# Thirty-two columns of an adaptation vector moved from VectorE and GpSimd to TensorE, in a hybrid decoder layer

## The chip, the cores and the metric

The program runs on one core of a Trainium2 chip. A core has five engines that run side by side, each with its own in-order queue: PE (TensorE, matrix products), DVE (VectorE), ACT (ScalarE), POOL (GpSimd) and SP (SyncE, which here only issues DMAs). They meet through semaphores. The metric is device time in microseconds (us) of one launch, the median of several runs.

## What is computed

One layer of a decoder trunk, for one sequence of 1024 tokens and a model width of 1024, all in float32. Cut to what matters here:

```
c_act = silu(c)                                  # 1024 values
mod = c_act @ w_ada + b_ada                      # w_ada is 1024 x 6144
shift1, scale1, gate1, shift2, scale2, gate2 = split(mod, 6)
h = rms_norm(x, norm1_w) * (1 + scale1) + shift1
proj = h @ w_in                                  # delta-rule heads and window heads
... gated delta rule (chunked, triangular solve) and sliding-window attention ...
x = x + gate1 * (concat(o_g, o_s) @ w_out)
h2 = rms_norm(x, norm2_w) * (1 + scale2) + shift2
x = x + gate2 * ((silu(h2 @ w_gate) * (h2 @ w_up)) @ w_down)
```

The adaptation vector `mod` has 6144 values. The kernel keeps it as 48 columns of 128 values in a tile `modc` (128 x 48): columns 0 to 15 are shift1 and scale1, which the very first stage needs; columns 16 to 47 are gate1, shift2, scale2 and gate2, which are needed much later (gate1 first, after the output projection).

## The kernel before, in words

Activations lie transposed, with the 1024 features as 8 tiles of 128 partitions and the tokens along the free axis, in two halves of 512. Each dense product is done as three fp32r products (the weight and the activation are each split into a high and a low part), so one *dense step* is three matmuls of 128 x 512, and a unit is eight such steps into one PSUM bank; a *skv* unit has steps of three matmuls 128 x 272. The generator `dense` hands out these steps; `fill(n)` puts n of them into PE's queue. PE's order is written out by hand (`manual_schedule`), the other engines' order is set by a scheduler when the program is built.

The order of the work, and the stretches that the prediction names:

- **Start.** Columns 0 to 15 of `modc` on DVE (`start_col`, L438), norm 1 and the first units.
- **Stretch A.** The rest of `h` (`modulate1`, L330 to L337: POOL, ACT and DVE), and a loop of 14 rounds, each with `fill(6)` and two columns of `modc` by `ada_some`: one by POOL (L256, a product of 128 x 1024) with a summing copy on ACT (L257), one by DVE alone (L253, a product with sum, 128 x 1024). A small DVE add of the bias (L259) follows each. Every column first needs its 512 KB of `w_ada`, loaded by SP into rings of two buffers with the tags b, c, d and e. Meanwhile DVE does the causal convolutions of the dense units (`conv`, L363 to L371: three long sums that read PSUM, three short ones for the seam L371, and the `tails` copy L368), which free the PSUM banks. A ends when PE reaches `psg` (L666), the cumulative sum of the decays, whose input `tsc` DVE makes (L641 to L661).
- **Stretch B.** The four head pairs (`pair_gen`), with dense steps between their visits.
- **Stretch C.** The triangular solve on DVE (`solve`, L817 and L820, about 60 short operations in a chain), with the window queries' norms between them; in it also the last four of the 32 columns (three on POOL, one on DVE).
- **After C.** `merge` and `scan_chunk`, the attention, the output projection and the feed-forward part.

The bank helper `sm` turns over four PSUM banks; `t2` is a ring of three 128 x 512 scratch tiles; `t4` gives the 512 KB tiles.

Of the kernel before, what the change touches and what calls it, by code (L numbers as in the profile page):

```python
# [54 lines left out]
def tile_hybrid_layer(  # L55
# [4 lines left out]
    rowvec: bass.AP,  # L60
    ada: bass.AP,
    wmain: bass.AP,
    wskv: bass.AP,
# [56 lines left out]
    def bc(ap, shape):  # L120
        return ap.broadcast_to(list(shape))
# [123 lines left out]
    def load_ada(u, tag=None):  # L245
        adat[u] = t4(f"ada{u}", tag=tag)
        done["ada"] = sp.dma_start(out=adat[u], in_=ada[u])

    def mod_col(u, eng=dve, bias=True):

        w = adat.pop(u)
        if eng is dve:
            dve.tensor_tensor_reduce(out=w, in0=w, in1=cb, scale=1.0, scalar=0.0, op0=ALU.mult, op1=ALU.add,  # L253
                                     accum_out=modc[:, u:u + 1])
        else:
            eng.tensor_tensor(out=w, in0=w, in1=cb, op=ALU.mult)  # L256
            act.activation(out=w, in_=w, func=AF.Copy, accum_out=modc[:, u:u + 1])  # L257
        if bias:
            dve.tensor_tensor(out=modc[:, u:u + 1], in0=modc[:, u:u + 1], in1=b_ada[:, u:u + 1], op=ALU.add)  # L259

    ada_next = [16]

    def ada_some(n, tag, eng=dve):
        for u in range(ada_next[0], ada_next[0] + n):
            if "kd" in done:
                with tc.issue_after(done["kd"].ins):
                    load_ada(u, tag)
            else:
                load_ada(u, tag)
            mod_col(u, eng)  # L270
        ada_next[0] += n

# [617 lines left out]
    def val(p):  # L890
        run(value_gen(p))

    for i in range(ADA_ITER):
        fill(VISITS_A[0])
        with tc.issue_after(h_done[0].ins), tc.issue_after(h_done[1].ins):
            ada_some(1, ADA_TAGS[2 * i], pool if i not in ADA_DVE else dve)
            ada_some(1, ADA_TAGS[2 * i + 1])
    next(token)
# [47 lines left out]
    for n, visit in zip(VISITS_B, (v0, v1, v2, v3, q0, q0, q1, q1, q2)):  # L946
        fill(n)
        next(visit)
        if visit is v3:
            for i in range(32 - 2 * ADA_ITER):  # L950
                ada_some(1, "b", pool if i % 4 else dve)
    dve.scalar_tensor_tensor(out=a2, in0=modc[:, 32:40], scalar=1.0, in1=n2w, op0=ALU.add, op1=ALU.mult)
# [701 lines left out]
```

## Time and profile before

| | |
|---|---|
| median of 3 runs | 1319.54 us (1319.52, 1319.54, 1326.32) |
| the profiled execution | 1316.65 us, its span 1314.9 us |
| PE, DVE, ACT, POOL busy share of the span | 91%, 68%, 41%, 48% |
| mean granted TensorE clock | 0.96 |

The span runs from the first to the last instruction; 1.75 us lie around it. Shares over the whole span hide the stages: from about 345 us on PE is nearly always busy, before that DVE is. PE records of a fp32 matmul come in twos (two passes), those of a fp32r matmul alone. A granted clock of 1.00 is 2.4 GHz, 0.50 is 1.2 GHz, and what lies between is a mean over a stretch.

### The profile page before, as it was taken

The numbers are of one execution on the slowest core, as the hardware profiler recorded it, in microseconds if no ns is written. First come the engines' busy times: TensorE is split into PE (matmuls) and PEld (weight loads), VectorE is DVE, ScalarE is ACT, GpSimd is POOL, SyncE is SP. The second block draws the span as 40 slices with busy tenths as digits, with TensorE's granted clock in tenths as the row PEclk, the third lists the DMA queues.
The fourth block names the chain that finished last, engine by engine and source line by source line (L and its number), as shares of the span: only waits on it lengthen the run. The fifth ranks groups of instructions, "written<-read, shape, count | busy, mean of one in ns | idle before, by whom it ended". The sixth has DMA issues, their size and how long they took to land.

```text
span 1314.9 us, 18979 instructions
## 1 busy us (share of the span) xinstructions
PE 1192.7 (91%) x6710; PEld 974.5 (74%) x6710; DVE 892.6 (68%) x1690; ACT 538.8 (41%) x1028; POOL 629.4 (48%) x453
## 2 busy tenths in 40 slices
PE   6867697896999799997998999999999999999998
PEld 5757576684788678785786788777777888888887
DVE  7999989979724677576646416877876875546430
ACT  4373555422434777434356432222232334544430
POOL 4667344534335444344354455545455545455440
PEclk8899799898999899998899999999999999999999
DMA  8727468485639865366845625556665567775651
GB/s 326 233 85 273 144 132 227 133 229 183 199 126 205 132 113 165 106 218 216 288 157 187 207 95 203 208 200 228 212 212 201 176 217 281 250 252 195 201 168 40
DMA packets 167214, 250.62 MB, mean 191 GB/s; under 512 B 40656, under 2 KB 106448, under 8 KB 165584
## 3 DMA queue, kind: packets, MB, share of 16 engines
q1 hardware_dynamic: 157520, 241.03, 56.6%
q0 software_dynamic: 9600, 8.39, 3.9%
q8 instruction: 53, 0.87, 0.3%
q14 instruction: 41, 0.34, 0.1%
HBM read 182.89 MB, written 66.45 MB: 190 GB/s over the span
## 4 chain that ended last, share of the span: by engine, by line
PE 43%; DVE 16%; DMA 8%; issue 4%; POOL 3%; ACT 3%; SPq 0%; DVEq 0%; ACTq 0%; POOLq 0%
PE ps_P L1359 5%; PE ps_P L1358 5%; PE ps_P L1360 5%; DMA wb<-in_wgate_dram 4%; PE ps_S L1358 2%; PE ps_S L1359 2%; PE ps_S L1360 2%; PE ps_c L1358 2%; PE ps_c L1359 2%; POOL wS L193 2%; PE ps_c L1360 2%; DVE wa L1427 1%; PE ps_gz L212 1%; DMA SD<-sd 1%; DVE soltmp L817 1%
## 5 line engine op out<-in xcount | busy, mean ns | idle before, releaser
L193 POOL TENSOR_TENSOR wP<-rP,wP 128x512 fp32r<-128x512 f32 (+1 forms) x84 | 108.3, 1301 | 105.3 <-ACT wP L192 100.2
L1359 PE MATMUL ps_P<-t,wP 128*128 128x512 f32 x308 | 120.4, 391 | 0.0
L1358 PE MATMUL ps_P<-t,wP 128*128 128x512 f32 x308 | 120.4, 391 | 0.0
L1360 PE MATMUL ps_P<-t,wP 128*128 128x512 f32 x308 | 120.2, 390 | 0.0
L193 POOL TENSOR_TENSOR wS<-wa,wS 128x512 fp32r<-128x512 f32 x44 | 62.8, 1437 | 111.8 <-ACT wS L192 78.9
L1360 PE MATMUL ps_S<-T,wS 128*128 128x512 f32 x264 | 102.8, 390 | 0.3 <-POOL wS L193 0.3
L1359 PE MATMUL ps_S<-T,wS 128*128 128x512 f32 x264 | 102.9, 390 | 0.0
L1358 PE MATMUL ps_S<-T,wS 128*128 128x512 f32 x264 | 102.9, 390 | 0.0
L192 ACT ACTIVATE wP<-rP 128x512 fp32r<-128x512 f32 (+1 forms) x84 | 48.4, 590 | 77.6 <-PE ps_P L1360 49.2
L1358 PE MATMUL ps_c<-B,w 128*128 128x512 f32 x176 | 70.5, 401 | 6.1 <-ACT X L1398 6.1
L1360 PE MATMUL ps_c<-B,w 128*128 128x512 f32 x176 | 69.7, 396 | 0.0
L1359 PE MATMUL ps_c<-B,w 128*128 128x512 f32 x176 | 69.7, 396 | 0.0
L1465 ACT ACTIVATE sg<-sg 128x512 f32<-128x512 f32 x33 | 20.9, 632 | 116.0 <-DVE sg L1461 116.0
L1358 PEld LDWEIGHTS ps_P<-t,wP 128*128 128x128 f32 x308 | 57.9, 188 | 12.6
L1360 PEld LDWEIGHTS ps_P<-t,wP 128*128 128x128 f32 x308 | 57.9, 188 | 12.5
L1359 PEld LDWEIGHTS ps_P<-t,wP 128*128 128x128 f32 x308 | 57.8, 188 | 12.4
L192 ACT ACTIVATE wS<-wa 128x512 fp32r<-128x512 f32 x44 | 26.7, 624 | 94.6 <-DVE wa L1426 71.8
L1424 DVE TENSOR_TENSOR ws<-wb 128x512 f32<-128x512 f32 x22 | 23.1, 1051 | 62.1 <-DMA wb<-in_wgate_dram 54.5
L1360 PEld LDWEIGHTS ps_S<-T,wS 128*128 128x128 f32 x264 | 49.6, 188 | 11.1 <-POOL wS L193 0.7
L212 PE MATMUL ps_o<-mix,w_o 128*128 128x512 f32 x128 | 53.7, 420 | 4.2 <-ACT w_o L192 4.2
L1358 PEld LDWEIGHTS ps_S<-T,wS 128*128 128x128 f32 x264 | 49.6, 188 | 10.5
L1359 PEld LDWEIGHTS ps_S<-T,wS 128*128 128x128 f32 x264 | 49.6, 188 | 10.5
(507 smaller groups left out, 3559.4 us busy)
## 6 DMA issues: line engine op xcount, KB each, us to landing
ada<-in_ada_dram SPq DMA_DIRECT2D x48, 512.0 KB, 4.7
AD<-ops SPq DMA_DIRECT2D x11, 1536.0 KB, 5.0
rP<-SD SPq DMA_DIRECT2D x16, 704.0 KB, 5.7
sd<-in_wdown_dram SPq DMA_DIRECT2D x20, 512.0 KB, 5.3
SD<-sd SPq DMA_DIRECT2D x20, 512.0 KB, 3.9
rP<-in_wdown_dram SPq DMA_DIRECT2D x12, 704.0 KB, 5.3
XD<-X SPq DMA_DIRECT2D x22, 256.0 KB, 3.3
xu<-XD SPq DMA_DIRECT2D x22, 256.0 KB, 3.4
```

The costliest lines, as they stand in the source:

```text
L192: act.activation(out=r(hi), in_=src, func=AF.Copy)
L193: last = eng.tensor_tensor(out=r(lo), in0=src, in1=hi, op=ALU.subtract)
L212: pe.matmul(out, lhsT=r(lhs[0]), rhs=r(rhs[0]), start=first, stop=False)
L817: dve.tensor_tensor(out=tv[g], in0=bc(L[:, i, i + 1:32].unsqueeze(1), (P, i, 31 - i)), in1=bc(L[:, 0:i, i:i + 1], (P, i, 31 - i)), op=ALU. ...
L1358: pe.matmul(ps, lhsT=r(wh), rhs=r(xh), start=first and i == 0, stop=False, **kw)
L1359: pe.matmul(ps, lhsT=r(wh), rhs=r(xl), start=False, stop=False, **kw)
L1360: pe.matmul(ps, lhsT=r(wl), rhs=r(xh), start=False, stop=i == n - 1, **kw)
L1424: dve.tensor_tensor(out=s1, in0=a21, in1=a22, op=ALU.add)
L1427: dve.tensor_tensor(out=a12, in0=a12, in1=a11, op=ALU.subtract)
L1465: act.activation(out=out, in_=out, func=AF.Silu)
```

## The change

All 32 columns go to PE. Four columns make a group: `ada_gen` issues, for each of its 4 column tiles, 8 fp32 matmuls with 32 stationary columns (the same column of `c` 32 times over) and 128 moving ones; matmul k goes to the column group k mod 4 of the array (`tile_position`), so PSUM holds four partial sums, in partitions 0, 32, 64 and 96. ACT copies the bank to a scratch tile (`ada_row`), and four matmuls with one moving column (`sel`, 1 in those four partitions) add the four sums up and turn the row into columns; one DVE add puts in the bias for all four. A group is done in four steps (two tiles of matmuls, two more, the copy, the sums), and the loop takes three steps after each `fill(6)` from the fourth round on. All 32 loads of `w_ada` are set out ahead of the loop; the weights lie in DRAM in the layout of the other weights, 4 KB in a piece as before.

```diff
+    sel = cp.tile([P, 1], F32, name="sel")
+    pool.memset(sel, 0.0)
+    for g in range(4):
+        pool.memset(sel[32 * g:32 * g + 1], 1.0)
     ada_next = [16]
-    def ada_some(n, tag, eng=dve):
-        for u in range(ada_next[0], ada_next[0] + n):
-            ...
-                load_ada(u, tag)
-            mod_col(u, eng)
+    def ada_load(tag):
+        ...
+        adat[u] = t4(f"ada{u}", (P, KT, P), tag=tag)
+        with tc.issue_after((done["kd"] if "kd" in done else done["x"]).ins):
+            sp.dma_start(out=adat[u], in_=ada2[u - 16])
+    def ada_gen(u0, q=None):
+        ps = sm(f"ps_ada{u0}", q)
+        for m in range(2):
+            for n in (2 * m, 2 * m + 1):
+                w = adat.pop(u0 + n)
+                for k in range(KT):
+                    g = k % 4
+                    pe.matmul(ps[32 * g:32 * g + 32, n * P:(n + 1) * P], lhsT=bc(c_col[:, k:k + 1], (P, 32)), rhs=w[:, k],
+                              start=k < 4, stop=k >= 4, tile_position=(0, 32 * g))
+            yield
+        row = t2(f"ada_row{u0}")
+        act.activation(out=row, in_=ps, func=AF.Copy)
+        yield
+        for n in range(4):
+            pe.matmul(ps[:, n:n + 1], lhsT=row[:, n * P:(n + 1) * P], rhs=sel, start=True, stop=True)
+        dve.tensor_tensor(out=modc[:, u0:u0 + 4], in0=ps[:, 0:4], in1=b_ada[:, u0:u0 + 4], op=ALU.add)
+        yield
...
+    adas = chain(*(ada_gen(16 + 4 * i) for i in range(8)))
+    for tag in ADA_TAGS:
+        ada_load(tag)
     for i in range(ADA_ITER):
         fill(VISITS_A[0])
-        with tc.issue_after(h_done[0].ins), tc.issue_after(h_done[1].ins):
-            ada_some(1, ADA_TAGS[2 * i], pool if i not in ADA_DVE else dve)
-            ada_some(1, ADA_TAGS[2 * i + 1])
+        for _ in range(3 if i >= 3 else 0):
+            next(adas, None)
+    run(adas)
...
-        if visit is v3:
-            for i in range(32 - 2 * ADA_ITER):
-                ada_some(1, "b", pool if i % 4 else dve)
```

PE's queue in stretch A, inside the second half of the unit `gk2` (the key projection of pair 2), before:

```order
L212 MATMUL ps_gk2_1_855<-h2_132,w_gk2h_635 128x512
L213 MATMUL ps_gk2_1_855<-h2_132,w_gk2h_635 128x512
L214 MATMUL ps_gk2_1_855<-h2_132,w_gk2l_636 128x512
L212 MATMUL ps_gk2_1_855<-h3_133,w_gk2h_635 128x512
L213 MATMUL ps_gk2_1_855<-h3_133,w_gk2h_635 128x512
```

and after:

```order
L213 MATMUL ps_gk2_1_898<-h2_138,w_gk2h_641 128x512
L214 MATMUL ps_gk2_1_898<-h2_138,w_gk2h_641 128x512
L215 MATMUL ps_gk2_1_898<-h2_138,w_gk2l_642 128x512
L286 MATMUL ps_ada16_917<-ada16_760,sml_99 32x128 x8
L286 MATMUL ps_ada16_917<-ada17_762,sml_99 32x128 x8
L286 MATMUL ps_ada16_917<-ada18_764,sml_99 32x128 x8
L286 MATMUL ps_ada16_917<-ada19_766,sml_99 32x128 x8
L213 MATMUL ps_gk2_1_898<-h3_139,w_gk2h_641 128x512
L214 MATMUL ps_gk2_1_898<-h3_139,w_gk2h_641 128x512
```

Between two dense steps stand the 32 small matmuls of the first group (columns 16 to 19; `sml` holds `c`), and nothing else has moved on PE here: the dense steps keep their order.

At the end of the last skv unit two of the eight groups have their third and fourth step without dense steps between them; after the change PE's queue reads there (the group of columns 36 to 39; `gk0_1` is the next dense unit):

```order
L215 MATMUL ps_skv7_1242<-wk_hi_154,h3_139 128x272
L286 MATMUL ps_ada36_1256<-ada38_804,sml_99 32x128 x8
L286 MATMUL ps_ada36_1256<-ada39_806,sml_99 32x128 x8
L293 MATMUL ps_ada36_1256<-sel_130,ada_row36_1310 128x1 x4
L213 MATMUL ps_gk0_1_1322<-h0_136,w_gk0_1_1317 128x512
```

The sums (L293) read `ada_row36`, which ACT makes from the two rows just above.

POOL's queue in stretch A before (`xt` are the last products of `modulate1`, `w_` the splits of weights):

```order
L334 TENSOR_TENSOR xt6_1_567<-xt6_1_567,row_n1_1_684 128x512
L256 TENSOR_TENSOR ada16_776<-ada16_776,cb_119 128x1024
L256 TENSOR_TENSOR ada20_846<-ada20_846,cb_119 128x1024
L256 TENSOR_TENSOR ada22_874<-ada22_874,cb_119 128x1024
L256 TENSOR_TENSOR ada18_811<-ada18_811,cb_119 128x1024
L256 TENSOR_TENSOR ada26_947<-ada26_947,cb_119 128x1024
L256 TENSOR_TENSOR ada34_1067<-ada34_1067,cb_119 128x1024
L256 TENSOR_TENSOR ada28_977<-ada28_977,cb_119 128x1024
L193 TENSOR_TENSOR w_gq0_1_1153<-w_gq0_1r_1154,w_gq0_1_1153 128x1024
```

and after:

```order
L358 TENSOR_TENSOR xt6_1_573<-xt6_1_573,row_n1_1_690 128x512
L194 TENSOR_TENSOR w_gq0_1_1390<-w_gq0_1r_1391,w_gq0_1_1390 128x1024
L194 TENSOR_TENSOR w_gk1_1_1467<-w_gk1_1r_1468,w_gk1_1_1467 128x1024
L194 TENSOR_TENSOR w_gq1_1_1546<-w_gq1_1r_1547,w_gq1_1_1546 128x1024
L194 TENSOR_TENSOR w_gk3_0_1658<-w_gk3_0r_1659,w_gk3_0_1658 128x1024
```

Only the four splits of weights are left to POOL in the rest of A.

## Rows read from the trace of the kernel before

**Rows 1.** Stretches A and C: length; PE, PEld, DVE, ACT, POOL busy; clock, DMA.

```profile
77.20:157.70 80.50, 53.07 (x260) 44.97 (x259) 79.91 (x126) 40.31 (x80) 50.62 (x22) 0.87 0.52 183
...
285.40:345.00 59.60, 43.84 (x206) 35.95 (x204) 59.04 (x171) 15.23 (x25) 22.83 (x14) 0.89 0.58 182
```

**Rows 2.** Waits of PE, 77 to 346 us: us in total, times, longest.

```profile
PE psr_s L725 <- ACT wide_s L721: 15.0, 2, 13.4
PE psg L666 <- DVE tsc L661: 12.1, 1, 12.1
...
PE ps_gk L212 <- ACT kq L387: 8.6, 1, 8.6
```

**Rows 3.** Timeline, 85 to 97 us: start, duration, engine, line, operation [idle before, releaser].

```profile
85.00 5.17 POOL L256 TENSOR_TENSOR ada<-ada,cb 128x1024 f32<-128x1024 f32 x2
...
85.12 5.59 DVE L332 SCALAR_TENSOR_TENSOR h<-xt,modc,h 128x512 fp32r<-128x512 f32 x2
...
92.61 0.74 DVE L332 SCALAR_TENSOR_TENSOR h<-xt,modc,h 128x512 fp32r<-128x512 f32 x1
...
96.93 0.77 PE L212 MATMUL ps_gk<-h,w_gk2h 128*128 128x512 f32 x1 [8.59 <-ACT kq L387]
```

**Rows 4.** PE in A by group of instructions, and its timeline: dense matmuls back to back.

```profile
L213 PE MATMUL ps_skv<-wk_lo,h 128*128 128x272 f32 x33 | 10.1, 306 | 0.0
...
103.93 0.39 PE L212 MATMUL ps_gq<-h,w_gq 128*128 128x512 f32 x1
104.16 0.39 PE L213 MATMUL ps_gq<-h,w_gq 128*128 128x512 f32 x1
...
112.02 0.29 PE L212 MATMUL ps_skv<-wk_hi,h 128*128 128x272 f32 x1
112.14 0.29 PE L213 MATMUL ps_skv<-wk_lo,h 128*128 128x272 f32 x1
```

**Rows 5.** Timeline of PE at fp32 matmuls with two column groups, and with none.

```profile
71.22 0.95 PE L321 MATMUL ssps<-ones,sq 128*128 128x1 f32 x8
...
197.40 2.37 PE L781 MATMUL psA<-kq,kn 64*64 64x128 f32 x59
...
212.02 1.09 PE L781 MATMUL psA<-kq,kn 64*64 64x128 f32 x16 [0.16 <-ACT sq_q L710]
213.04 0.50 PE L212 MATMUL ps_gv<-h,w_gv 128*128 128x512 f32 x1
...
362.48 1.16 PE L1039 MATMUL pk<-S,kvq 128*128 128x128 f32 x8
```

**Rows 6.** Timeline of ACT in A.

```profile
109.90 0.67 ACT L363 ACTIVATE qt<-ps_gq,sml 128x512 f32<-128x512 f32 x1
110.47 1.05 ACT L192 ACTIVATE w_gq<-w_gq_1r 128x1024 fp32r<-128x1024 f32 x1
...
132.88 1.28 ACT L643 ACT_TABLE_LOAD   x1
```

**Rows 7.** DMA issues by line: count, KB each, median us to landing.

```profile
ada<-in_ada_dram SPq DMA_DIRECT2D x48, 512.0 KB, 4.7
```

**Rows 8.** Timeline of PE just behind `psg`.

```profile
160.46 0.63 PE L213 MATMUL ps_gk<-h,w_gk 128*128 128x512 f32 x1
```

**Rows 9.** Timeline of POOL and DVE in C.

```profile
306.19 1.21 DVE L253 CUSTOM_DVE_ANT_0 ada<-ada,cb 128x1024 f32<-128x1024 f32 x1
...
311.42 0.38 DVE L820 TENSOR_TENSOR lanes<-lanes,soltmp 128x234 f32<-128x234 f32 x1
...
311.58 5.00 POOL L256 TENSOR_TENSOR ada<-ada,cb 128x1024 f32<-128x1024 f32 x2 [10.41 <-DVE soltmp L817]
...
312.33 2.00 DVE L820 TENSOR_TENSOR lanes<-lanes,soltmp 128x234 f32<-128x234 f32 x1
...
314.25 2.59 DVE L817 TENSOR_TENSOR soltmp<-lanes 128x238 f32<-128x238 f32 x1
...
320.46 2.34 DVE L184 TENSOR_TENSOR rsq_s<-rsq_s 128x16 f32<-128x16 f32 x1
```

More of the change, by code (lines that the diff above doesn't have):

```diff
@@ L61, in tile_hybrid_layer @@
     ada: bass.AP,
+    ada2: bass.AP,
     wmain: bass.AP,
@@ L259, in mod_col @@
             dve.tensor_tensor(out=modc[:, u:u + 1], in0=modc[:, u:u + 1], in1=b_ada[:, u:u + 1], op=ALU.add)
+    sel = cp.tile([P, 1], F32, name="sel")
+    pool.memset(sel, 0.0)
+    for g in range(4):
+        pool.memset(sel[32 * g:32 * g + 1], 1.0)
     ada_next = [16]
-    def ada_some(n, tag, eng=dve):
-        for u in range(ada_next[0], ada_next[0] + n):
-            if "kd" in done:
-                with tc.issue_after(done["kd"].ins):
-                    load_ada(u, tag)
-            else:
-                load_ada(u, tag)
-            mod_col(u, eng)
-        ada_next[0] += n
+    def ada_load(tag):
+        u = ada_next[0]
+        ada_next[0] += 1
+        adat[u] = t4(f"ada{u}", (P, KT, P), tag=tag)
[18 more added lines that the diff above has]
+        yield
     def rstd(ps, name):
@@ L1632 @@
         "rowvec": _np.concatenate([f["a_log"][0], f["dt_bias"][0], f["sinks"][0]]),
-        "ada": w_ada.T.reshape(48, P, D),
+        "ada": w_ada[:, 0:2 * D].T.reshape(16, P, D),
+        "ada2": tiles(w_ada[:, 2 * D:]),
         "wmain": tiles(_np.concatenate([w_in[:, 512:1024], w_in[:, 0:512], w_in[:, 1024:2048], w_in[:, 2064:2576]], axis=1)),
```

## The prediction

> **What bounds the kernel now.** I read the windows by stretch first, then PE's waits, then the timelines where a wait ends. In stretch A (77.2 to 157.7 us, up to `psg`) DVE is busy 79.9 of 80.5 us while PE is busy 53.1 and idle 27.4; in stretch C (285.4 to 345 us) DVE is busy 59.0 of 59.6 [rows 1]. So both are DVE's, and the reader is to see that POOL and ACT are not full in either. PE's long waits say the same: 12.1 us for `tsc` at the end of A, 8.6 us in A for a bank, 13.4 us in C for `wide_s`, whose input DVE makes [rows 2]. From 345 us on PE is busy nearly all the time, in an order that stays: what A and C gain or lose goes through to the end. Between them (stretch B) nothing is taken out.
>
> DVE's time in A is more than its own work. While POOL ran two of the `ada` products (5.17 us), two DVE operations with two SBUF inputs took 5.59 us together; one alone takes 0.74 [rows 3]. In C it is the same: beside POOL's products three short DVE operations took 2.00, 2.59 and 2.34 us, where one of the kind takes 0.38 [rows 9]. A POOL product thus costs DVE time as well as its own.
>
> **Stretch A after the change.** DVE loses its 14 products, most of its 28 bias adds and 14 POOL products beside it, so it stops being the limit, and A becomes a sum over PE's queue.
>
> Dense work: of the 260 PE records in A about 98 are of the 272-wide kind (33 on one of three lines), so 162 are 512 wide [rows 1, 4]. Back to back they follow each other at 0.2275 us (103.93 to 104.16, the mean over the units) and 0.126 us (112.02 to 112.14) [rows 4]. 162 x 0.2275 + 98 x 0.126 = 49.2 us, and 1.0 us for a stretch at the lower clock behind the wait that stays.
>
> The small matmuls: 256 fp32 matmuls, 512 records, in 16 steps of 32. The trace has none with four column groups; `psA` has the nearest: two column groups of 64. There a bank of 16 records, so eight rounds of two, took 1.02 us from its first start to the next dense matmul (212.02 to 213.04); `pk`, with no groups, took 1.16 us for eight records [rows 5]. With four groups running together a step of 32 is eight rounds of four, so again 1.02 us, and 0.1 us more for the restart of the dense matmuls behind it (0.50 against 0.39 in the row at 213.04 [rows 4, 5]): 1.12. Six steps follow another without dense work between and save 0.2 each: 16 x 1.12 - 1.2 = 16.7 us. Bounds: two groups at a time give 1.02 + 0.87 more a step (eight further rounds of 0.109, which is 1.02 less some 0.15 of start, over eight), 30.6 us; no overlap at all, at 1.16/8 = 0.145 a record, 74 us; below, rounds of four with no start and no restart, 512/4 x 0.109 = 14.0 us. The longest run of `psA`, 59 records in 2.37 us, 0.040 each [rows 5], would give 20.6. I take 16.7, from the single bank, the row nearest in shape to a step.
>
> The Trainium skill ("TensorE: Matmul & The Clock Gate", part 3 on packing) gives 2.38 times for three column tiles, not three; as an estimate from that page, four would give about 3.2, and the 16 steps 3.5 us more. No row here shows four tiles. The same page (steps of a matmul, decode) speaks of about 62 ns per matmul when the sequencer decodes in microcode; as an estimate from it the 512 records could not take less than 32 us, which would make this slower. The trace does not agree: 40 ns a record in `psA` [rows 5].
>
> The sums: four matmuls with one moving column are what `ssps` is, 0.95 us for eight records [rows 5]: 8 x 0.95 = 7.6 us.
>
> Waits of PE that stay or come. The bank wait at 96.93 ends when DVE has got through the operations stalled by POOL; without two products, and a third beside a `modulate` step, DVE is about 5.0 us earlier, and 8.6 - 5.0 = 3.6 us stay [rows 3]. New is PE's wait for ACT's copy; everything dense stands behind it in PE's queue. For six groups dense steps lie between, about 4.1 us (18 x 0.2275) or 2.3 us in skv (18 x 0.126). For the groups of columns 24 and 36 none do: the copy (about 0.65, as the 512-wide 0.67 [rows 6]) and hand-overs cost 0.9; and at column 36 a table load of 1.28 [rows 6] and the skv copies stand ahead of it on ACT, 2.5. At columns 20 and 44 a weight split of 1.05 and a 0.67 copy [rows 6] stand ahead on ACT while only two dense steps cover it: 1.7 and 1.3. Together 6.4 us. The bounds are 0 and, should the copy also queue behind a Silu that waits for DVE, about twice that.
>
> The loads are the same 512 KB each, landing 4.7 us after issue [rows 7]; they now wait for PE to release buffers six to eight tiles back, and four move up from C, ahead of two weight loads on SP. A group takes PE 2 x 1.12 + 0.95 and its dense steps, 6 to 8 us, so a load issued six tiles ahead is there; cost nothing, and if that cover goes, a landing less the cover, some 1 us a step.
>
> Sum: 49.2 + 1.0 + 16.7 + 7.6 + 3.6 + 6.4 = 84.5, against 80.5: A is 4.0 us longer. It also no longer ends in a wait of 12.1 us, behind which PE ran at the lower clock (0.63 a matmul instead of 0.39, about seven of them [rows 4, 8], 1.2 GHz against 2.4): 1.4 us back. `tsc` is off the path then: its inputs are there after the last skv unit, some 25 us of PE work ahead of `psg`.
>
> **Stretch C after the change.** It loses one DVE product (1.21), three short adds with it (0.3 together) and three POOL products. The stalls beside those fall from 2.00, 2.59 and 2.34 to about 0.4, 0.4 and 0.2 [rows 9]: 1.6 + 2.2 + 2.1. Together 7.4 us, all on the solve's chain; PE's 13.4 us wait [rows 2] shrinks with it, and the solve's result, which `merge` waits for, comes as much earlier. POOL's split of `w_sq` in the same place stays and goes on stalling DVE once.
>
> **Stretch B** is taken as unchanged. The scheduler has reordered DVE there (convolutions of `gk3` earlier), with the same operations; I allow 3 us either way.
>
> **Sum:** +4.0 - 1.4 - 7.4 = -4.8 us on the profiled execution, 1316.65 to 1311.9; on the median of the runs shown, 1319.54, that is 1314.7. I forecast 1315 us.
>
> **Rivals.**
> *Two groups at a time (slower).* The array takes only two of the four column groups together. For it: the rows show no more than two column groups. Against: nothing in them shows the second group costing the first anything. A step costs 1.89 us and PE 13.9 us more: -4.8 + 13.9 = +9, 1329 us. It decides from a step of about 1.4 us on, where A's loss eats C's gain. With no overlap at all, +52, 1372 us.
>
> *Loads late.* PE stands for `w_ada` in most of the 16 steps, about 1 us in 8 of them; DMA is at 0.52 of its time in A [rows 1], which speaks against. +3, 1323 us: no change that can be told.
>
> *PE's own waits do not come (faster).* ACT, which loses about 17 us in A and C, makes the copies in time, and the bank wait goes with DVE's relief: 6.4 + 3.6 us less, and A is shorter than before. For it: ACT is busy only half of A [rows 1]. Against: ACT's order has the splits ahead. -15, 1305 us; half of it, -10, 1310.
>
> *No gain from C.* PE reaches `merge` no earlier because other work in C holds it. PE's 13.4 us wait speaks against. Then +3, 1322 us.
>
> **How the numbers follow.** The measurement can tell about 0.5%, 6.6 us, from no change. Chances: forecast with its own spread (1311 to 1319) 0.40; two groups 0.19, no overlap 0.03; loads late 0.06; no gain from C 0.06; PE's waits gone 0.26. Faster by over 0.5% (under 1312.9): the last and a little of the forecast, 0.30. Slower (over 1326.1): 0.22 and a little, 0.24. Between: 0.46. The range 1304 to 1331 takes in the full rival of each sign.
>
> **What would show it.** In the profile after: the 32 records of a step in about 0.9 us and nearly 17 us for all 16 (right) or 1.7 us a step (two groups); PE idle in A about 10 us, with `ada_row` as releaser, and no wait for `tsc`; DVE no longer full in A; in C no DVE operation of 2 us at `soltmp` and `lanes` but one or two, the wait for `wide_s` near 6 us; the stretch from the first window query to `merge` earlier by A's change less 7. Wrong would be: A longer by over 10 us, a PE wait for `ada` loads, or a stretch B that changes by more than 3 us.

## The result, and the profile after

The changed kernel takes 1333.2 us (median of 8 runs, 1329.2 to 1340.3) against 1319.5 us of the kernel before in the same comparison (8 runs, 1317.3 to 1327.7): a ratio of 1.0092, 95% interval 1.0063 to 1.0121 (worked out from all the runs; it is not the ratio of the two medians). It is slower by 0.9%, where 1315 us and 1304 to 1331 were forecast. The profiled execution of after is one of 1329.16 us with a span of 1326.1 us, 12.5 and 11.2 us more than the one of before.

All lines of the kernel are 1 (at the top) to 24 further down than before, so L213 to L215 are the dense matmuls, L286 the small matmuls of `w_ada`, L290 the copy `ada_row`, L293 the sums. The page's line of busy time:

```profile
PE 1217.0 (92%) x7286; PEld 997.6 (75%) x7286; DVE 848.6 (64%) x1636; ACT 525.2 (40%) x1002; POOL 594.9 (45%) x441
```

DVE, ACT and POOL all have less to do, PE 576 records more (512 small, 64 of the sums). The stretches A, B and C by windows, after (columns as in [rows 1]), each from the first instruction of the stretch to that of the next. B and C meet here at the last unit of `psA`, and C goes to `merge`, so C begins earlier and ends later than in [rows 1]:

```profile
76.40:165.90 89.50, 80.23 (x836) 68.21 (x835) 40.67 (x83) 31.58 (x61) 14.87 (x8) 0.92 0.52 185
165.90:285.90 120.00, 94.95 (x601) 77.44 (x599) 101.24 (x178) 55.57 (x83) 52.78 (x24) 0.91 0.60 154
285.90:360.80 74.90, 67.55 (x371) 55.49 (x370) 64.73 (x194) 20.27 (x30) 34.01 (x21) 0.95 0.68 194
```

and B and C of before, cut at the same instructions:

```profile
157.70:271.90 114.20, 97.99 (x598) 80.31 (x598) 101.14 (x184) 56.65 (x84) 52.70 (x24) 0.91 0.62 161
271.90:353.90 82.00, 66.21 (x372) 54.77 (x372) 72.10 (x200) 23.60 (x36) 33.90 (x24) 0.92 0.65 195
```

In A DVE falls from 79.9 us of work to 40.7, and yet A grows from 80.5 to 89.5 us; PE is now busy 80 of it. B grows by 5.8 us with the same work, C shrinks by 7.1. `merge` starts 6.9 us later (360.8 against 353.9), so 4 us more are lost behind it, where nothing was changed.

PE's waits in A after, and the timeline of PE at the first group and at the longest wait:

```profile
PE ps_ada L293 <- ACT ada_row L290: 5.7, 4, 2.6
PE ps_gk L213 <- DVE tails L392: 3.6, 1, 3.6
```

```profile
96.99 1.95 PE L286 MATMUL ps_ada<-ada,sml 128*32 128x128 f32 x64
98.87 0.50 PE L213 MATMUL ps_gk<-h,w_gk2h 128*128 128x512 f32 x1
...
139.66 1.55 PE L293 MATMUL ps_ada<-sel,ada_row 128*128 128x1 f32 x8 [2.61 <-ACT ada_row L290]
141.07 0.77 PE L213 MATMUL ps_gk<-h,w_gk 128*128 128x512 f32 x1
141.64 0.63 PE L214 MATMUL ps_gk<-h,w_gk 128*128 128x512 f32 x1
142.06 0.63 PE L215 MATMUL ps_gk<-h,w_gk 128*128 128x512 f32 x1
```

The 64 records of two steps take 1.88 us to the next dense matmul: the four column groups run side by side. The waits are those forecast, 3.6 and 5.7 us. But behind the wait of 2.61 us the sums take 1.55 us where 0.95 is usual, and the dense matmuls show 0.63 each and follow each other at 0.43 us (141.64 to 142.06), where [rows 4] has 0.39 and 0.23: the lower clock, as in [rows 8]. The granted clock is 0.50 from 140.0 to 146.9 us; before that it is 0.50 from 92.3 to 95.7 us, behind the bank wait, and from 112.7 to 116.2 us, behind an `ada_row` wait of 1.46 us. Behind the other two `ada_row` waits, of 0.8 and 0.9 us, it stays at 1.00.

All kernels of this study in one table. A runs from the first `ps_gk` of the unit gk2_0 to `psg`, B to the last unit of `psA`, C to `psm`, the first matmul of `merge`; then comes scan and attention, to the last `psS`; 119 to 124 us later, in every kernel, the feed-forward part begins with the first `ps_c`. Microseconds of the profiled execution; time and ratio are from all runs beside the kernel before on the same chip. That kernel's own median was 1319.5 to 1322.7 us there, so kernels of different comparisons are compared by their ratios. Before and after have two profiles.

| kernel | median | ratio (95%) | A | B | C | `merge` at | scan | feed-f. | PE records |
|---|---|---|---|---|---|---|---|---|---|
| before | 1319.5 | | 80.5, 80.3 | 114.2, 114.0 | 81.9, 82.4 | 353.9, 354.3 | 171.8, 175.1 | 667.0, 667.4 | 6710 |
| after | 1333.2 | 1.0092 (1.0063-1.0121) | 89.5, 89.7 | 119.9, 121.5 | 75.0, 75.0 | 360.8, 365.2 | 177.5, 175.9 | 668.6, 674.2 | 7286 |
| b_order | 1331.6 | 1.0058 (1.0030-1.0086) | 86.3 | 115.8 | 75.0 | 354.8 | 177.1 | 675.2 | 7286 |
| a_dummy | 1321.4 | 0.9996 (0.9969-1.0022) | 85.4 | 116.2 | 75.0 | 356.6 | 175.3 | 671.4 | 7354 |
| a_cover | 1328.5 | 1.0058 (1.0025-1.0090) | 86.5 | 117.4 | 74.8 | 357.7 | 176.1 | 674.2 | 7286 |
| a_cover2 | 1326.7 | 1.0043 (1.0017-1.0069) | 78.8 | 115.4 | 75.0 | 346.7 | 177.8 | 677.2 | 7286 |
| c_only_p | 1326.6 | 1.0050 (1.0021-1.0080) | 82.2 | 119.1 | 79.0 | 357.7 | 176.6 | 674.3 | 6782 |
| hold | 1334.5 | 1.0094 (1.0061-1.0126) | 89.4 | 114.1 | 74.7 | 355.6 | 184.2 | 672.9 | 7286 |
| hold_dummy | 1320.2 | 0.9975 (0.9949-1.0001) | 83.4 | 111.4 | 75.0 | 347.1 | 177.5 | 667.7 | 7354 |
| hold_cover | 1319.4 | 0.9984 (0.9958-1.0009) | 78.1 | 112.0 | 75.0 | 342.6 | 179.8 | 673.2 | 7286 |
| hybrid | 1311.4 | 0.9912 (0.9882-0.9943) | 71.5 | 117.3 | 74.9 | 342.4 | 178.2 | 666.8 | 6998 |
| hold_hybrid | 1311.4 | 0.9916 (0.9880-0.9951) | 78.2 | 110.6 | 75.0 | 341.9 | 176.4 | 669.6 | 6998 |
| best | 1315.5 | 0.9962 (0.9931-0.9992) | 71.8 | 115.2 | 74.8 | 339.0 | 187.6 | 673.7 | 6998 |
| before_split | 1322.5 | 0.9995 (0.9968-1.0022) | 79.7 | 112.1 | 82.3 | 351.8 | 179.1 | 668.9 | 6710 |
| before_sel | 1321.7 | 1.0008 (0.9982-1.0034) | 80.3 | 114.3 | 81.8 | 353.6 | 175.5 | 665.3 | 6710 |
| hold_one | 1331.8 | 1.0080 (1.0045-1.0116) | 89.9 | 111.4 | 75.0 | 356.1 | 182.1 | 676.2 | 7286 |
| before_72 | 1328.5 | 1.0045 (1.0019-1.0071) | 80.4 | 113.6 | 82.5 | 356.1 | 174.9 | 672.2 | 6782 |
| hold_68 | 1327.4 | 1.0042 (1.0013-1.0072) | 90.0 | 115.6 | 75.0 | 359.4 | 174.9 | 672.4 | 7354 |

"Lost at the lower clock" below is worked out from windows of 2 us: PE's busy time in each with a granted clock under 0.97, times one minus that clock, summed over the stretch.

### The profile page after: what moved, and what is told of

Read it like the earlier page. It is cut to its first block, busy times and chain, and to the rows that moved or that the text cites. A ratio compares the mean times of both kernels' runs of the same rounds, so it can differ in the third digit from the quotient of the medians.

```text
span 1326.1 us, 20037 instructions
## 1 busy us (share of the span) xinstructions
PE 1217.0 (92%) x7286; PEld 997.6 (75%) x7286; DVE 848.6 (64%) x1636; ACT 525.2 (40%) x1002; POOL 594.9 (45%) x441
## 3 DMA queue, kind: packets, MB, share of 16 engines
q1 hardware_dynamic: 157520, 241.03, 55.7%
## 4 chain that ended last, share of the span: by engine, by line
PE 44%; DVE 15%; DMA 8%; issue 3%; POOL 3%; ACT 2%; SPq 0%; DVEq 0%; ACTq 0%; POOLq 0%
PE ps_P L1382 5%; PE ps_P L1384 5%; PE ps_P L1383 5%; DMA wb<-in_wgate_dram 3%; PE ps_S L1382 2%; PE ps_S L1383 2%; PE ps_S L1384 2%; PE ps_c L1382 2%; PE ps_c L1384 2%; PE ps_c L1383 2%; POOL wS L194 2%; DMA SD<-sd 1%; DVE soltmp L841 1%; PE ps_gz L213 1%; PE ptr L1070 1%
## 5 line engine op out<-in xcount | busy, mean ns | idle before, releaser
L194 POOL TENSOR_TENSOR wP<-rP,wP 128x512 fp32r<-128x512 f32 (+1 forms) x84 | 109.3, 1313 | 103.8 <-ACT wP L193 98.6
L1383 PE MATMUL ps_P<-t,wP 128*128 128x512 f32 x308 | 119.9, 389 | 0.0
L1382 PEld LDWEIGHTS ps_P<-t,wP 128*128 128x128 f32 x308 | 57.8, 188 | 12.1
L193 ACT ACTIVATE wS<-wa 128x512 fp32r<-128x512 f32 x44 | 26.6, 623 | 93.4 <-DVE wa L1450 86.3
L1448 DVE TENSOR_TENSOR ws<-wb 128x512 f32<-128x512 f32 x22 | 24.8, 1129 | 60.4 <-DMA wb<-in_wgate_dram 54.5
L1384 PEld LDWEIGHTS ps_S<-T,wS 128*128 128x128 f32 x264 | 49.6, 188 | 11.2 <-POOL wS L194 0.7
L213 PE MATMUL ps_o<-mix,w_o 128*128 128x512 f32 x128 | 52.6, 411 | 4.3 <-ACT w_o L193 4.3
```

The costliest lines, as they stand in the source:

```text
L193: act.activation(out=r(hi), in_=src, func=AF.Copy)
L194: last = eng.tensor_tensor(out=r(lo), in0=src, in1=hi, op=ALU.subtract)
L213: pe.matmul(out, lhsT=r(lhs[0]), rhs=r(rhs[0]), start=first, stop=False)
L1382: pe.matmul(ps, lhsT=r(wh), rhs=r(xh), start=first and i == 0, stop=False, **kw)
L1383: pe.matmul(ps, lhsT=r(wh), rhs=r(xl), start=False, stop=False, **kw)
L1384: pe.matmul(ps, lhsT=r(wl), rhs=r(xh), start=False, stop=i == n - 1, **kw)
```

## The experiments

### A second profile of each

No edit.

> The kernel before, once more, for a second profile of it: the parts up to merge should agree with the first within 2 us, and the part from the first psO on (881.2 us in the first, against 887 to 893 us in four of the changed kernels) tells whether the first was a lucky one. Theory (the late part only draws a different number of stretches at 1.2 GHz each time): 881 to 892 us. Rival (the late part is longer in every kernel with the change): 881 us within 1.5 us again.

> The changed kernel, once more, for a second profile: stretch A 88 to 90 us again, with the 5.7 us of waits for ada_row and the low stretch behind the longest of them, B 119 to 121 us with the three waits of psr_k, C 75 us. If A or B differ by more than 2 us from the first profile, the reading of them needs a range.

Stretches A, B and C repeat within 0.5 us in before and 1.6 us in after; A loses 3.4 and 5.5 us at the lower clock before, 6.9 and 6.3 after. The later parts do not repeat in after (668.6, 674.2; 3.2 and 7.9 us of it lost at the lower clock), nor does the scan in before (171.8, 175.1). So a difference of several us in A to C is read from one profile, and one of 5 us behind `merge` is not.

### Stretch B: the order on VectorE, and why it changed

In B, PE's waits for `psr_k` (L725 before, L749 after), before, after and in hold:

```profile
PE psr_k L725 <- ACT wide_k L721: 9.9, 2, 7.5
```

```profile
PE psr_k L749 <- ACT wide_k L745: 17.1, 3, 7.0
```

```profile
PE psr_k L749 <- ACT wide_k L745: 11.8, 2, 7.6
```

After has a third wait, and the timeline of DVE shows what it waits for: `fk`, the end of pair 0's norm, from which `wide_k` is made.

```profile
199.90 0.74 DVE L389 SCALAR_TENSOR_TENSOR kn<-ps_gk,sml,kn 128x511 f32<-128x511 f32 x1
...
201.99 0.74 DVE L389 SCALAR_TENSOR_TENSOR kn<-ps_gk,sml,kn 128x510 f32<-128x510 f32 x1
...
204.01 0.74 DVE L389 SCALAR_TENSOR_TENSOR kn<-ps_gk,sml,kn 128x509 f32<-128x509 f32 x1
...
206.45 0.16 DVE L779 TENSOR_TENSOR fk<-rn,ed 128x16 f32<-128x16 f32 x1
```

The long sums of the key convolutions of pair 3 (L389) stand between the short steps of the norm. b_order holds them back by hand:

```diff
+        late.append(rest) if p == 3 else rest()
...
+            if visit is p0 and ("rows", "k0") in done:
+                with tc.issue_after(done["rows", "k0"].ins):
+                    while late:
+                        late.pop(0)()
```

> The changed kernel with one thing put back: VectorE does the two key convolutions of pair 3 behind the scaling of pair 0's keys, as in the kernel before, and not ahead of the second norm. Theory (the scheduler's new order in stretch B costs 7.0 us): the 7.04 us wait of PE for wide_k at 206.6 us is gone or under 1.5 us, the stretch from psg to the last psA goes from 119.9 back to 114 to 116 us, and the time from 1333 to 1325 to 1328 us. Rival (VectorE has as much to do in B either way, the wait only moves): the three psr_k waits and the psA and ps_kd waits together stay at 21 us or more, and the time stays at 1331 to 1335 us.

The middle wait goes and B falls to 115.8 us, as the theory said. The time misses what was expected: the ratio falls from 1.0092 to 1.0058, some 4.5 us, with intervals that overlap; 1325 to 1328 us had been expected, and 1331.6 is the rival's. Why the scheduler had moved the convolutions, hold tells. The last products of C read `cb` (the vector `c` spread over a 128x1024 tile); without them its buffer, one of six in a ring, is free early, and pair 3's key tile, which takes one of that ring, can be written earlier.

```diff
+        if visit is v3:
+            pool.tensor_tensor(out=modc[:, 0:1], in0=cb[:, 0:1], in1=rnq[:, 3, 0, 0:1], op=ALU.mult)
```

> The changed kernel with one short GpSimd operation more (128x1, in stretch C, in the place of the products that were there): it reads the tile cb, the 512 KB in which the product columns had their second factor, so that cb's buffer stays taken until C as in the kernel before. No order is set by hand; VectorE's order in stretch B then comes out as in the kernel before, row by row. Theory (the change let cb's buffer go early, one of six in that ring; so the key tile of pair 3 got a buffer earlier and its two convolutions moved ahead of pair 0's norm on VectorE): the waits for psr_k in B fall from 17.1 to 10 us, B is 113.5 to 115.5 us instead of 119.9 and 121.5, A and C stay at 89.6 and 75.0, and the time is 1324 to 1329 us. Rival (B is longer for another reason, the loads or the clock): B 118 us or more and the time 1331 us or more.

With one operation of 128x1 that keeps `cb` until C, B is 114.1 us, as before. DVE in hold:

```profile
201.62 0.19 DVE L187 SCALAR_TENSOR_TENSOR rn<-rsq_g 128x32 f32<-128x32 f32 x1
201.85 0.17 DVE L779 TENSOR_TENSOR fk<-rn,ed 128x16 f32<-128x16 f32 x1
201.94 1.28 DVE L751 TENSOR_TENSOR kn<-kn,psr_k 128x512 f32<-128x512 f32 x2
```

`fk` comes at 201.9 and the norm is not cut up, although `psg` was 0.8 us later. B's loss is thus shown to be a freed buffer, not the matrix engine. The time did not follow: all four runs of hold take 1330 to 1335 us, where 1324 to 1329 were expected, and the ratio is after's, though `merge` starts 5 to 10 us earlier than in after. In the profile the gain is gone by the end of the scan, which lost 17.8 us at the lower clock (184.2 us), where all but one of the other kernels lost 2 to 14; hold_one, which differs from hold only in where `w_ada` lies, lost 9.5 there and took 1331.8 us. So what B lost is explained, but no run shows that giving it back alone makes the kernel faster.

### Stretch A: PE's waits and the clock behind them

a_dummy (on b_order) and hold_dummy (on hold) put 68 transposes that nobody reads into PE's five waits of A:

```diff
+    def dummy(n, u0):
+        if n:
+            ps = sm(f"dum{u0}", 0 if u0 in (16, 20, 36) else 3)
+            for _ in range(n):
+                pe.transpose(out=ps[:, 0:P], in_=ident, identity=ident)
...
+        dummy({20: 6, 24: 10, 36: 18, 44: 6}.get(u0, 0), u0)
         for n in range(4):
             pe.matmul(ps[:, n:n + 1], lhsT=row[:, n * P:(n + 1) * P], rhs=sel, start=True, stop=True)
...
+        if i == 2:
+            dummy(28, 16)
```

> As b_order, and in the five places of stretch A where PE waits (for a bank at 87.5 us, for ada_row in the groups of columns 20, 24, 36 and 44) 28, 6, 10, 18 and 6 transposes that nobody reads, at about 0.12 us each, so that PE is busy through most of each wait. Nothing else moves. Theory (PE's short waits are followed by stretches at 1.2 GHz, which lost 1.7, 1.7 and 3.4 us): those three low stretches go, psg starts 5 to 7 us earlier than in b_order (at 159 to 161 us), and the time is 5 to 7 us under b_order's. Rival (the low stretches come from the small matmuls or from something else than the waits): they stay, psg starts where it does in b_order within 1.5 us or later, by up to 2 us where transposes outlast the wait, and the time is b_order's or 2 us more.

> As hold, with the 28, 6, 10, 18 and 6 idle transposes of a_dummy in PE's five waits of stretch A. Theory (1.2 GHz follows the waits): A is 84 to 86.5 us against 89.6, with under 2.5 us lost at the lower clock against 6.3 and 6.9, and the time 3 to 6 us under hold's. Rival: A within 1.5 us of hold's.

a_dummy ran 10 us under b_order, but its profile shows only part of that in A (85.4 against 86.3: b_order's A lost 3.4 us where after's lost 6.9, for no lower clock followed its bank wait), and 3.4 us at 1.2 GHz (116.0 to 119.4 us) stayed in a_dummy; `psg` came at 165.4 us, where 159 to 161 had been expected. hold_dummy is clean: A 83.4 us against 89.4, nothing lost at the lower clock. The time is 14 us less on the medians, so more than A's 6.0; the profiles have the rest in B, the scan and the feed-forward part. The place of the longest wait there (`dum` are the transposes):

```profile
135.08 2.19 PE L282 MATMUL dum<-ident 128*128 128x128 f32 x18
137.76 1.05 PE L300 MATMUL ps_ada<-sel,ada_row 128*128 128x1 f32 x8 [0.50 <-ACT ada_row L296]
138.67 0.48 PE L213 MATMUL ps_gk<-h,w_gk 128*128 128x512 f32 x1
138.99 0.40 PE L214 MATMUL ps_gk<-h,w_gk 128*128 128x512 f32 x1
```

```profile
77.40:160.80 83.40, 81.32 (x905) 70.69 (x904) 40.73 (x83) 31.66 (x61) 14.88 (x8) 1.00 0.55 198
```

The copy comes no earlier, yet the sums take 1.05 us and the dense matmuls show 0.40, not 0.63. Useless work made the kernel faster: the waits themselves cost 9.3 us, and in A what followed them 6 more.

The cover kernels take the waits away. The copy goes with the second step, and three dense steps lie between any two steps; the first group stands in the bank wait:

```diff
-        fill(VISITS_A[0])
-        for _ in range(3 if i >= 3 else 0):
-            next(adas, None)
-    run(adas)
+        for j in range(2):
+            fill(3)
+            for _ in range(2 if (i, j) == (2, 1) else int(i > 3 or (i, j) == (3, 0))):
+                next(adas, None)
```

> As b_order, but stretch A's steps are spread: the copy on ScalarE goes with the second step of matmuls, every group is three steps, three dense steps lie between any two of them, and the two matmul steps of the first group stand in the wait for a bank at 87.5 us. The same work on every engine. Theory (A's surplus is PE's own waits and what the clock loses behind them): the waits for ada_row fall from 5.7 us to under 1, the bank wait from 3.6 to 1.5 or less, at most one low stretch stays, and psg starts at 150 to 155 us instead of 165.9; the time is 10 to 14 us under b_order's, about 1313 to 1317 us. Rival (VectorE's convolutions, in whose queue the bias adds now wait for PE's sums, bound A): bank waits come in place of the others, psg starts at 161 us or later, and the time is within 4 us of b_order's.

> As a_cover, but the ring buffers are dealt out so that the first group's four weight tiles are in the two rings that are free early (order of rings b, c, c, b for it, then d, d); a_cover's PE waited 7.9 us for the third tile. Theory (PE's queue and its waits bound A): the 7.9 us wait goes, A (from the unit gk2_0 to psg) is 76 to 79 us instead of 86.5, and the time is 1318 to 1322 us. Rival (VectorE, through the bank at the first gk2_1, holds PE anyway): a bank wait of 5 us or more comes in its place, A 83 us or more, and the time stays at 1326 to 1330 us.

> As hold, with the steps of stretch A spread as in a_cover2 (whose A was 78.8 us with nothing lost at the lower clock). Theory (the change's loss is A's waits with the clock behind them, and B's order): A 78 to 80 us, B 114 to 116, C 75, merge starts 6 to 9 us earlier than in the kernel before, and the time is 1313 to 1319 us: the change as meant, faster than before by 0.2 to 0.6%. Rival (PE's queue behind merge gives it back, as a_cover2 lost 13 us there): merge as early, the time 1320 us or more.

a_cover ran into a wait of its own, for the third weight tile of the first group, whose buffer the input tokens hold until `modulate1` is through:

```profile
PE ps_ada L286 <- DMA ada<-in_ada_dram: 7.9, 1, 7.9
```

Its A (86.5 us) and time (1328.5, where 1313 to 1317 were expected) missed for it. With the rings dealt out anew (`"bccbdd" + "bcd" * 3` in place of `"bcd" * 5`) A is 78.8 and 78.1 us, the full clock throughout (hold_cover):

```profile
77.50:155.60 78.10, 75.66 (x836) 62.27 (x834) 40.66 (x82) 31.59 (x61) 14.96 (x8) 1.00 0.61 212
```

That is 11 us under after with the same instructions, and `merge` starts 11 us earlier than before. But a_cover2's time is 1326.7 us, where 1318 to 1322 were expected, and hold_cover's is 0.998 of before's (0.9958 to 1.0009): 1319.4 us, just over the 1313 to 1319 expected, and not shown to be faster than before. In hold_cover's profile 5 to 8 us come back in the scan and 6 in the feed-forward part.

### Stretch C alone

The kernel before with columns 44 to 47 alone on PE, in C (and b_order's hold-back):

```diff
-                ada_some(1, "b", pool if i % 4 else dve)
+                ada_load(u)
+        if visit in (q0, q1):
+            next(last)
```

> The kernel before with only the four columns of stretch C (44 to 47) moved to PE, in the layout and by the matmuls of the change, in stretch C beside the window queries; the 28 of stretch A stay on VectorE and GpSimd, and pair 3's key convolutions are held behind pair 0's scaling as in b_order. Theory (the gain of C, 6.9 us between the last psA and merge, is there by itself): stretch A as before (psg at 157 to 158 us), psm starts 5 to 8 us earlier than before's 353.9, and the time is 1311 to 1315 us against 1319.5. Rival (what C gains is given back later, as the changed kernel lost 4 us behind merge): psm as early, but the time within 3 us of 1319.5.

C fell only to 79.0 us, since PE now waited for the loads:

```profile
PE ps_ada L279 <- DMA ada<-in_ada_dram: 8.3, 1, 8.3
```

The theory failed (1326.6 us, and `psm` at 357.7, no earlier than before), so C's gain is not shown by itself. The wait that C's gain came from, the 15.0 us for `wide_s` of [rows 2], is a third of that in after:

```profile
PE psr_s L749 <- ACT wide_s L745: 5.1, 2, 4.7
```

C is 74.7 to 75.0 us in all thirteen kernels that have no ada work left there. What shrinks is what was forecast: in the 82 us up to `merge` before has 9 DVE operations of over 1.5 us, 20.2 us together; in the 75 us after there are 6, with 13.9.

### Behind merge: where the tensors lie, and PE's number of instructions

Behind `merge` every queue has in after the same instructions in the same order as before, with the same semaphores in the feed-forward part, and that part is still longer in most changed kernels. DVE's wait there for `wb`, a weight tile of 512 KB, tells two things. Its total goes with the length of the part: 51.5 to 54.5 us in the seven profiles of 665 to 669 us, 55.7 to 60.0 in ten of the eleven of 672 us and more. Its longest goes by the kernel and not by the length: 8.2 us in after at 668.6. Its rows for before, after, hold, before_72 and hold_68 (total, times, longest):

```profile
DVE ws L1424 <- DMA wb<-in_wgate_dram: 54.5, 11, 7.0
```

```profile
DVE ws L1448 <- DMA wb<-in_wgate_dram: 54.5, 11, 8.2
```

```profile
DVE ws L1450 <- DMA wb<-in_wgate_dram: 58.8, 11, 8.4
```

```profile
DVE ws L1425 <- DMA wb<-in_wgate_dram: 56.0, 11, 7.5
```

```profile
DVE ws L1454 <- DMA wb<-in_wgate_dram: 55.7, 11, 7.7
```

Three kernels move data and no work: `w_ada` as two DRAM tensors in the kernel before, as one in hold, and the tile `sel` in the kernel before.

```diff
-        "ada": w_ada.T.reshape(48, P, D),
+        "ada": w_ada[:, 0:2 * D].T.reshape(16, P, D),
+        "ada2": w_ada[:, 2 * D:].T.reshape(32, P, D),
```

> The kernel before with one thing of the change that is no instruction: w_ada lies in DRAM as two tensors (16 columns, 8 MB, and 32 columns, 16 MB, both in the old layout) and not as one of 24 MB. Every queue has the same instructions in the same order. Theory (where the tensors lie in DRAM sets how the feed-forward part's transfers meet): that part (first ps_c to the end) is 670 to 676 us as in the changed kernels, against 667.0 and 667.4, the longest wait of VectorE for wb 8.2 us or more against 7.0 and 7.1, and the time is 3 to 8 us over before's. Rival (the late part only draws more or less of the lower clock each time): 667 to 669 us, the wait 7.1, the time within 2 us of before's.

> The kernel hold with w_ada in DRAM as one tensor of 24 MB as in the kernel before (the last 32 columns in the new layout in it); every queue as in hold. Theory (place in DRAM): the feed-forward part 667 to 669 us against 672.9 in hold, the longest wait for wb 7.1 us, the time 4 to 8 us under hold's 1334.5. Rival: 671 us or more and the time within 3 us of hold's.

> The kernel before with only the small tile sel of the change and its five GpSimd memsets at the start, which nobody reads; it moves every later tile in SBUF by its size. Theory (place in SBUF sets the feed-forward part): 670 to 676 us for it, the wait for wb 8.2 us, the time 3 to 8 us over before's. Rival (place in DRAM, or the draw): 667 to 668 us, the wait 7.1, the time within 2 us of before's.

All three keep the time of the kernel they come from (0.9995, 1.0080, 1.0008), so these moves in DRAM and SBUF are not it, to within some 0.3%. A suspect that is left is PE's number of records. before_72 puts 72 idle transposes into the 12.1 us wait for `tsc`, hold_68 puts 68 into the longest wait of B (`keep_warm` issues transposes of `ident`):

```diff
+    keep_warm(72)
     next(token)
```

> The kernel before with 72 idle transposes on PE in its 12.1 us wait for tsc ahead of psg (72 x 0.117 = 8.4 us, so they end before the wait does). PE then has 6782 records, as c_only_p had. In the traces so far the feed-forward part goes by PE's number of records: 6710 in four kernels: 665 to 669 us, longest wait for wb 6.8 to 7.1; 6998 in two: 667 to 670 and 7.0, 7.1; 7286 in eight: 669 to 677 and 8.2 to 8.5; 7354 in two: 668 and 671, 7.7 and 7.3; 6782 in one: 674 and 7.7. Theory (it is the number of PE instructions ahead of that part, whatever they do): the wait for wb 7.5 to 7.9 us and the part 671 to 676 us, though A and B are as before or 2 us shorter; time 1322 to 1328 us. Rival (it has to do with the moved work): 665 to 669 us and 6.8 to 7.1, and the time 1 to 3 us under before's, for the clock behind psg.

> As hold, with 68 idle transposes on PE in its longest wait in stretch B (7.6 us for psr_k of pair 1), so 7354 records on PE as in hold_dummy, but none in stretch A. Theory (number of PE instructions): A 89 to 90 us as in hold, the wait for wb 7.3 to 7.7 us against 8.4, the feed-forward part 667 to 671 against 672.9, the time 1326 to 1331 us against 1334.5. Rival (hold_dummy's late part was the draw): 672 us or more, 8.2 or more, and hold's time within 3 us.

before_72 has them end before the wait does:

```profile
144.73 8.03 PE L304 MATMUL warm<-ident 128*128 128x128 f32 x72
152.51 0.48 PE L212 MATMUL ps_gk<-h,w_gk 128*128 128x512 f32 x1
...
160.02 0.69 PE L666 MATMUL psg<-tsc,tribd 128*128 128x64 f32 x2 [4.53 <-DVE tsc L661]
```

A, B and C are as before (80.4, 113.6, 82.5), and still the time is longer by 7 us on the medians, 6 by the ratio. That is the theory's side, and so is the table's feed-forward part, 672.2 against 667 us. But from `merge` to the end its profile takes 967.4 us, and before_split's, with no instruction changed, 971.2 (before's 961.1 and 964.5), so one profile does not place the loss. hold_68 is mixed: the wait fell to 7.7 us and the ratio from 1.0094 to 1.0042 as expected, but the feed-forward part hardly (672.4 against 672.9); what the profiles differ in is the scan (174.9 against 184.2).

Nor are the transposes the only thing that changed in before_72. Its queues have 28 DVE operations, and some of ACT and POOL, in another order in the scan and attention (435 to 459 us). The same holds for most kernels of the table, with 16 to 74 DVE operations: only after, before_split and before_sel have the old order there, and hold_dummy and hybrid but for 3 operations. From `merge` to the end these five and before take 961 to 971 us, the others 967 to 983. No run separates this order from the number of PE's instructions. So it is shown that before_72 is slower, and not shown by what, nor in which part. The page of before and after counts blocks of instructions that DMA brings in:

```profile
q8 instruction: 53, 0.87, 0.3%
```

```profile
q8 instruction: 57, 0.93, 0.3%
```

0.87 MB in 53 packets are 16 KB each, and 6710 matmuls with as many weight loads are 253 instructions to a packet, so these look like PE's; more instructions ahead would move the blocks against the program. The Trainium skill ("Runtime: NRT & Kernel Launch", Instruction fetch mechanics) also has blocks of 16 KiB, 256 instructions, and calls the cost of their borders mostly hidden; no run here shows a border meeting a wait for `wb`, so this stays a suspicion.

### A version that beats both

Since A was PE's sum and DVE idle for half of it, hybrid leaves every second group of four columns on DVE (1.21 us a product, none on POOL):

```diff
-    adas = chain(*(ada_gen(16 + 4 * i) for i in range(8)))
+    adas = chain(*(ada_gen(16 + 8 * i) for i in range(4)))
...
+        if i in (3, 4, 6, 7, 9, 10, 12, 13):
+            with tc.issue_after(h_done[0].ins), tc.issue_after(h_done[1].ins):
+                for _ in range(2):
+                    mod_col(next(on_dve))
```

> As a_cover2, but only four of the eight groups (columns 16 to 19, 24 to 27, 32 to 35, 40 to 43) are on PE; the other 16 columns are products on VectorE, 1.21 us each, none on GpSimd. VectorE is busy only 41 of 86 us in stretch A of a_cover. Theory (A is PE's sum in the changed kernel, and VectorE has room for 16 products): PE's share falls by 8 steps of 0.97 and 4 sums of 0.95, 11.6 us, and A is 65 to 69 us; psg starts at 142 to 147 us, and the time is 1306 to 1312 us, under the kernel before. Rival (weights land one per 1.6 us, or VectorE's products stand ahead of convolutions that free banks): A 75 us or more, the time 1317 us or more.

> As hold_cover, but with the 16 columns of hybrid on VectorE and 16 on PE, and the groups of PE half a round to a round later than in hybrid, where PE waited 5.6 us for a weight tile. Theory: that wait is under 1 us, A 64 to 68 us (71.5 in hybrid), B 114 to 116 (117.3 in hybrid), C 75; time 1300 to 1307 us. Rival (B and what follows it take back what A gains): A as expected but the time within 3 us of hybrid's 1311.4.

> hybrid's stretch A with hold's tile cb kept to stretch C in place of the order set by hand: 16 columns on PE, 16 on VectorE, none on GpSimd; 6998 records on PE. Theory: A 70 to 73 us, B 110 to 115, C 75, so merge starts at 334 to 341 us, the feed-forward part 667 to 670; time 1303 to 1309 us. Rival (part of it is given back between merge and the output projection, as in hybrid and hold_hybrid): merge as early, the time 1309 to 1313 us.

hybrid is faster than before by 0.9% (0.9912, 0.9882 to 0.9943), at the time expected. A is 71.5 us, above the 65 to 69 expected, with a wait of 5.6 us for a weight tile in it:

```profile
78.60:150.20 71.60, 64.23 (x549) 54.20 (x548) 57.47 (x125) 28.59 (x55) 13.26 (x8) 0.95 0.63 228
```

```profile
PE ps_ada L287 <- DMA ada<-in_ada_dram: 5.6, 1, 5.6
PE ps_gk L213 <- DVE tails L394: 1.8, 1, 1.8
```

Later groups and the buffer of `cb` kept (hold_hybrid) only moved the wait for weights (5.1 us in two): A is 78.2 us, not 64 to 68, B gained what A lost, and the time (1311.4) missed the 1300 to 1307 expected. best has hybrid's A and the earliest `merge` (339.0), as expected, and still takes 1315.5 us, more than theory and rival allowed. Its profile is of the slowest of its ten runs and lost 25 us at the lower clock in the scan; its feed-forward part (673.7 us with a wait of 7.1) also does not fit the count of records. Why an earlier `merge` does not come through there stays open.

## Why the prediction was wrong

- **The small matmuls: right, a little dear.** 1.12 us a step was forecast, two take 1.88 and one alone 1.0 to the next matmul; 16 cost about 15.5 us, not 16.7. The rival of two groups at a time (1.89 a step) is false: 29 ns a record are a fifth of the 145 of `pk` [rows 5], which contain its start, and 3.8 times less than the 112 of the 72 transposes above, which are as wide and have no groups. The sums took the 0.95 us forecast at the full clock. Both sentences on the Trainium skill ("TensorE: Matmul & The Clock Gate", part 3 on packing: about 2.38 times for three column tiles; steps of a matmul: about 62 ns a matmul when the sequencer decodes in microcode) speak for more time than this; the measurement decides.
- **The waits: right.** Bank 3.6 us forecast and measured; `ada_row` 6.4 forecast, 5.7 measured, in the four groups named. So the rival "PE's own waits do not come" fell, and "loads late" too: no wait for weights stands among A's.
- **The low clock in A: the term that was mis-sized.** "1.0 us for a stretch at the lower clock behind the wait that stays" had no row; A lost 6.9 and 6.3 us in the two profiles, in after's first 1.7 behind the bank wait and 5.1 behind two of the `ada_row` waits. The forecast counted the 12.1 us wait's cost as given back (-1.4) and the new waits at their own length only, although [rows 8] showed what follows a wait. 49.2 + 6.9 + 15.5 + 7.7 + 3.6 + 5.7 = 88.6 of 89.5 us; hold_dummy, where the waits stay occupied, gives the 6 us back.
- **"Stretch B is taken as unchanged", 3 us either way: the step that failed.** It measured +5.7 and +7.5 us. The moved convolutions were seen, and taken as "the same operations"; they stood in front of the chain that PE waits for. The cause, `cb`'s buffer, lies in a part that the change only removes.
- **Stretch C: right, in size and in kind.** -7.4 us forecast, -6.9 and -7.4 measured; the long DVE operations give back 6.3 us, where 5.9 were forecast for the stalls, though more of them stay than the "one or two" expected. The rival "no gain from C" fell.
- **"What A and C gain or lose goes through to the end": wrong by several us.** After loses 4 to 6 us behind `merge` in the two pairs of profiles, and the feed-forward part is 1.6 and 6.8 us longer; in the scan the profiles lose 2 to 25 us at the lower clock. With `merge` only 1.5 us later than before, hold still takes 12 us longer by its ratio. What behind `merge` takes the time stays open.

Together: +9 in A, +6 to +7.5 in B, -7 in C, a start 0.8 us earlier or 1.6 later, so `merge` 7 to 11 us later where -4.8 was forecast. Of the 16 us between the forecast and the first profile's +11.2, A has 5.0, B 7.1 (the -1.4 was expected there), C 0.5, what is behind `merge` 4.3, and the start takes 0.8 off.

## What to carry to other kernels

When work moves onto the engine that sets the order, count a wait of it for its length and ask in the profile whether dense work at 1.2 GHz stands behind it (here behind three of five), and put steps so that three others lie between a product and its use. When a change removes the last reader of a tile, look at who takes its buffer next and where that work then stands in its queue. Split the work between the freed engine and the new one rather than move all of it. Instructions put in as a test can make the scheduler reorder other engines far behind them: compare the queues before the test is read as one change.

## What the runs showed of the hardware that was not expected

- Four column groups of 32 run side by side almost fully: 64 records in 1.88 us, 29 ns each, with 128 moving columns each, where transposes of that width without groups take 112 ns each (72 in 8.03 us).
- A wait of 2.61 us behind small matmuls was followed by 6.8 us at 1.2 GHz (140.0 to 146.9 us in after, 3.4 us lost) in all six profiles that have that wait (after twice, b_order, hold, hold_one, hold_68), and not in the two with 18 idle transposes in it. The bank wait of 3.6 us was followed by 3.4 us at 1.2 GHz in five of these six, and not in b_order.
